# Sums of quarters of a normed activation, made in three pieces between matrix products instead of in one block ahead of them

## Chip, cores and metric

The kernel runs on one core of a Trainium2 chip. The metric is the device time of one execution in microseconds. Its time before the change is 953.83 us, the median of 3 runs (953.82 to 955.91).

## The reference, cut

One decoder layer on x of 512 tokens by 1024 channels, in float32. The part around the change:

```
h = rms_norm(x, norm_mix)
z = h @ w_in                      # split: z_rnn z_q z_k z_v z_g z_dec z_mq z_gate
out_a = rg_lru(causal_dwconv(z_rnn), ...)          # branch 0
out_b = rms_norm(chunked_gla(z_q, z_k, z_v, ...)) * silu(z_g)   # branch 1
out_c = attention of z_mq over mem                 # branch 2
proj  = einsum(branches, w_branch)                 # 768 -> 1024, for each branch
gates = sigmoid(z_gate)
x = x + (sum over branches of gates * proj) @ w_out
...                               # then a gated MLP with a conv, and a final norm
```

z_v (with the 16 columns of z_dec) and z_g are each a product of h (512 x 1024) with 768 columns.

## The kernel before

**Exact products in two halves.** TensorE (PE in the profile) multiplies rounded float32. Each operand is therefore split into an upper part and a rest by `split` (lines 96 and 97): ScalarE (ACT) copies the source to a rounded tile (`whi`, `r`), and VectorE (DVE) subtracts that from the source (`wlo`, or again `r`). `mm3` (line 103) then makes three matmuls per term: upper by upper, upper by rest, rest by upper. The normed x lies channel-major in `hh` (upper) and `hl` (rest), both finished long before the change's place.

**The products for z_v and z_g** come from `seven`: seven products of quarters stand for the eight of a 2 x 2 by 2 x 2 block product. They are called a1, a2, c1, c2, b1, b2 and b3, each in two units (p = 0 and 1) of 12 matmuls, two token tiles by six. a1 and a2 add up in the same two PSUM banks, c1 and c2 in two others, b1 to b3 in two more. After a1, `v_read` copies the banks on ACT (line 790 in the profile) before a2 adds onto them. The quarter products c1, c2, b1 and b2 need sums and differences of quarters of h on one side: `h_sums(p)` makes them on DVE for one half of the channels (p). It adds `hh` and `hl` for four quarters (line 732), makes four combinations (lines 733 to 736), and splits four results: 12 DVE operations and 4 ACT operations of 512 columns. On the weights' side, sums are made by loads that add (issued by GpSimd, line 298); a plain load goes through SyncE's queue (lines 293 and 302).

**The branches.** Branch 2 comes first, then branch 0, then branch 1. For each of the 8 blocks d of output channels a branch has a gate unit (24 matmuls of 512 columns, then a sigmoid on ACT, line 619) and a projection unit (18 matmuls, then DVE operations, lines 625 to 628). In the list `b0` of branch 0 they alternate: gate 0, projection 0, gate 1, projection 1, and so on. Projections of branch 0 need all of `oa`, the output of the LRU: `lru_square`, `lru_root` (square roots on ACT, line 695), `lru_scan` (a scan on DVE, line 708, copies on ACT, line 716, and splits).

**Order.** The program is a list of units and of steps in between. `weave(units, steps)` spreads steps behind the units of a list; `blend(units, fast)` puts a share of the made units (those of `seven`) behind each unit. A unit has hooks with a lead m: the hook is called m units ahead of it, in `emit`. Weights are loaded and split by such a hook with a lead of two (`AHEAD`). The last steps woven into the last four units of branch 2 are `lru_square` for blocks 4 to 7, `lru_root(1)`, `lru_scan` for blocks 4 to 7, and `h_sums(0)`, `h_sums(1)`. Then `blend` puts four made units behind each of the first seven units of `b0`, the 14 of z_v and then the 14 of z_g. What comes out of this is the order in which operations are handed to a planner. It puts each engine's instructions in an order of its own by when it takes them to be ready, so an engine's order can depart from the program's; on the chip each engine works through its queue in order.

**Buffers.** PSUM gives 5 banks to the big products (`bank`). Split weights have 3 buffers each for upper and rest, raw weights 4, and the 53 slots of `apool` hold activations, among them the sums (`fslot`, `rslot`).

Of the kernel before, what the change touches and what calls it, by code (L numbers as in the profile page):

```python
# [8 lines left out]
F32 = mybir.dt.float32  # L9
# [5 lines left out]
ALU = mybir.AluOpType  # L15
# [3 lines left out]
P = 128  # L19
# [12 lines left out]
LOW = 16  # L32
# [9 lines left out]
HT = S // 2  # L42
# [14 lines left out]
def trunk(ctx: ExitStack, tc: tile.TileContext, x, xT, mem, memT, par, wdecay, wch, wv, wg, wmk,  # L57
          wmv, wrg, wbr, wout, wup, wdown, wdown2, gffn, gfin, out):
    nc = tc.nc
# [11 lines left out]
    def nm(s):  # L71
        uid[0] += 1
        return f"{s}_{uid[0]}"

    def fslot(shape=(P, S)):
        return apool.tile(list(shape), F32, tag="s", name=nm("f"))

    def rslot(shape=(P, S)):
        return apool.tile(list(shape), F32R, tag="s", name=nm("r"))
# [4 lines left out]
    def bank(shape=(P, S)):  # L84
        return psm.tile(list(shape), F32, tag="mm", name=nm("mm"))
# [8 lines left out]
    def split(hi, lo, src, eng=None):  # L94

        nc.scalar.activation(hi, src, AF.Copy)  # L96
        (eng or nc.vector).tensor_tensor(out=lo, in0=src, in1=hi.bitcast(F32), op=ALU.subtract)  # L97
# [34 lines left out]
    def unit(dram, n, fn, parts=1):  # L132

        w = {}
        i = sum(1 for k, *_ in prog if k == "unit")

        def ready():
            w["w"] = fetch(dram, n, parts)
            for h in behind.get(i, ()):
                h()  # L140
        prog.append(("unit", [(AHEAD, ready)], lambda: fn(w["w"])))

    def made_unit(pre, fn):

        prog.append(("unit", pre, fn))

    def step(fn):
        prog.append(("step", [], fn))

    def weave(units, steps, lead=0):  # L150

        done, m = 0, max(1, len(units) - lead)
        for i, u in enumerate(units):
            unit(*u)
            upto = len(steps) * max(0, i + 1 - lead) // m
            for s in steps[done:upto]:
                step(s)
            done = max(done, upto)
        for s in steps[done:]:
            step(s)  # L160
# [123 lines left out]
    def seven(src, n, np, lhs, pre, read, far=AHEAD):  # L284

        raw, w, banks = {}, {}, {}

        def load(q, p):  # L290
            raw[q, p] = [fslot((P, n)) for _ in range(2)]
            for j in range(2):
                loads.append(nc.sync.dma_start(raw[q, p][j], src(q, p)[:, j, :]))

        def add(to, q, p):

            for j in range(2):
                nc.gpsimd.dma_start(raw[to, p][j], src(q, p)[:, j, :], accum_op=ALU.add)  # L298

        def direct(q, p):  # L300
            raw[q, p] = wpool.tile([P, 2, n], F32, tag="raw", name=nm("raw"), bufs=NRAW)
            loads.append(nc.sync.dma_start(raw[q, p], src(q, p)))

        def ready(key, q, p):
            hi = wpool.tile([P, 2, n], F32R, tag="whi", name=nm("whi"))
            lo = wpool.tile([P, 2, n], F32R, tag="wlo", name=nm("wlo"))
            if isinstance(raw[q, p], list):
                for j in range(2):
                    split(hi[:, j, :], lo[:, j, :], raw[q, p][j])
            else:  # L310
                split(hi, lo, raw.pop((q, p)))
            w[key, p] = hi, lo

        def run(key, p):
            ws = w.pop((key, p))
            b = key[0]
            for i in range(2):
                if key[1] == "1" and p == 0:
                    banks[b, i] = bank((P, n))
                mm3(banks[b, i], [(*lhs(key, p, j, i), ws[0][:, j, :], ws[1][:, j, :]) for j in range(2)],  # L320
                    key[1] == "1" and p == 0, p == np - 1, key[1] != "1")
                if p == np - 1:
                    read(key, i, banks[b, i])

        steps = {
            "a1": ("B11", [(6, lambda p: load("B11", p))]),
            "a2": ("B21", [(far, lambda p: direct("B21", p))]),
            "c1": ("B11", [(6, lambda p: add("B11", "B12", p))]),
            "c2": ("B22", [(far, lambda p: direct("B22", p))]),
            "b1": ("B11", [(6, lambda p: add("B11", "B22", p))]),  # L330
            "b2": ("B12", [(10, lambda p: load("B12", p)), (7, lambda p: add("B12", "B22", p))]),
            "b3": ("B11", [(6, lambda p: add("B11", "B21", p))]),
        }
        us = []
        for key, (q, before) in steps.items():
            for p in range(np):
                us.append(([(m, lambda f=f, p=p: f(p)) for m, f in before] +
                           [(AHEAD, lambda key=key, q=q, p=p: ready(key, q, p))] +
                           [(m, lambda f=f, p=p: f(p)) for m, f in pre.get(key, ())],
                           lambda key=key, p=p: run(key, p)))  # L340
        return us

    def blend(us, fast, steps=()):

        for i, u in enumerate(us):
            unit(*u)
            for l, f in ((fast, lambda v: made_unit(*v)), (steps, step)):
                for v in l[len(l) * i // len(us):len(l) * (i + 1) // len(us)]:
                    f(v)
# [4 lines left out]
    hh = hpool.tile([P, KD, S], F32R, name="hh", tag="hh")  # L354
    hl = hpool.tile([P, KD, S], F32R, name="hl", tag="hl")
# [165 lines left out]
    def proj_in(i, evac):  # L521
        return wch[i], D, lambda w: evac(channel_major(w, KD, lambda k: (hh[:, k, :], hl[:, k, :])))
# [168 lines left out]
    def lru_root(g):  # L691
        with tc.issue_after(lru["last"].ins):
            for i in range(4):
                w = lru["aw", 4 * g + i][1]
                nc.scalar.activation(w, w, AF.Sqrt)
# [23 lines left out]
                split(*rr, of[t])  # L719
                oa.append(rr)  # L720


    hsum = {}

    def h_sums(p):

        tt = nc.vector.tensor_tensor
        f = {}
        for r, c in ((2, 1), (2, 2), (1, 1), (1, 2)):
            f[r, c] = fslot((P, 2, HT))  # L730
            a, b = (v[:, 4 * c - 4 + 2 * p:4 * c - 2 + 2 * p, (r - 1) * HT:r * HT].bitcast(F32) for v in (hh, hl))
            tt(out=f[r, c], in0=a, in1=b, op=ALU.add)
        tt(out=f[2, 2], in0=f[2, 1], in1=f[2, 2], op=ALU.subtract)
        tt(out=f[2, 1], in0=f[1, 1], in1=f[2, 1], op=ALU.subtract)
        tt(out=f[1, 1], in0=f[2, 2], in1=f[1, 1], op=ALU.subtract)
        tt(out=f[1, 2], in0=f[1, 2], in1=f[1, 1], op=ALU.add)
        for key, a in (("c1", f[2, 2]), ("c2", f[1, 2]), ("b1", f[1, 1]), ("b2", f[2, 1])):
            hsum[key, p] = rslot((P, 2, HT)), rslot((P, 2, HT))
            split(*hsum[key, p], a)

    def h_lhs(key, p, j, i):
        tk = slice(i * P, (i + 1) * P)
        if (key, p) in hsum:
            return tuple(a[:, j, tk] for a in hsum[key, p])
        k = 2 * p + j + (4 if key in ("a2", "b3") else 0)
        t = 2 + i if key == "b3" else i
        return hh[:, k, t * P:(t + 1) * P], hl[:, k, t * P:(t + 1) * P]

    each = lambda fn, bs: [lambda b=b: fn(b) for b in bs]
    lo, hi = range(4), range(4, 8)  # L750
    b2 = [u for d in range(KD) for u in branch(2, oc, d)]
# [5 lines left out]
    weave([lru_weights(1)] + b2[4:8], each(lru_square, lo) + [lambda: lru_root(0)] + each(lru_split, hi))  # L757
    weave(b2[8:12], [s for p in zip(each(lru_scan, lo), each(lru_gates, hi)) for s in p])
    step(lambda: lru_decay(1))
    weave(b2[12:], each(lru_square, hi) + [lambda: lru_root(1)] + each(lru_scan, hi) + each(h_sums, range(2)))  # L760


    HP = 2 * DV
# [10 lines left out]
    def causal():  # L774
        msk = fslot((P, NT, P))
        nc.gpsimd.memset(msk, 1.0)
        nc.gpsimd.affine_select(out=msk, in_=msk, compare_op=ALU.is_ge, fill=0.0, base=0, pattern=[[0, NT], [1, P]],
                                channel_multiplier=-1)
        nc.vector.tensor_copy(mki, msk)

# [48 lines left out]
            silu(i + 2, 0, d)  # L831

    def v_fast():
        return seven(lambda q, p: wv[p, int(q[1]) - 1, int(q[2]) - 1], HP + LOW, 2, h_lhs, {}, v_read, 4)

    def g_fast():
        return seven(lambda q, p: wg[p, int(q[1]) - 1, int(q[2]) - 1], HP, 2, h_lhs, {}, g_read, 4)
# [144 lines left out]
    b0 = [u for d in range(KD) for u in branch(0, oa, d)]  # L982
    gates = {}

    def hold(d):
        def evac(ps):
            gates[d] = fslot()
            nc.scalar.activation(gates[d], ps, AF.Sigmoid)
        return proj_in(18 + 8 + d, evac)

    held = [hold(d) for d in range(KD)]
    blend(b0[:7], v_fast() + g_fast())
    weave(b0[7:] + held[:2], [decay_in, qk_back] + [lambda h=h: decay_logit(h) for h in range(H)] + [decay_log] +
          [lambda h=h: decay_apply(h) for h in range(H)])
# [325 lines left out]
```

## Time and profile before

| | us |
|---|---|
| median of 3 runs | 953.83 |
| the profiled execution | 953.96 |
| its span | 952.3 |
| PE busy | 925.5 |
| DVE busy | 637.6 |
| ACT busy | 500.4 |

A row of the timeline has start and length in us, the engine, the line, the operation, output<-inputs with shape, the count of instructions merged into it, and in brackets the idle time of the engine ahead of it and what ended that. For a matmul the inputs are named as right operand, left operand. A row of the table by stretches has the stretch and its length, then busy time and count for PE, PE's weight loads, DVE, ACT and GpSimd, then the granted clock of PE (1.00 is full), the busy share of the DMA engines, and GB/s. The mean granted clock of the execution is 0.991.

### The profile page before, as it was taken

To read this page: it belongs to the slowest core of one execution; us is meant where nothing else is said; L and a number is where in the kernel's file an instruction comes from. 1 tells how busy PE (TensorE), PEld (TensorE's weight loads), DVE (VectorE), ACT (ScalarE), POOL (GpSimd) and SP (SyncE) were. 2 spreads that over 40 slices of the span, in tenths; PEclk is the share of its full clock that TensorE was granted. 3 is DMA by queue.
4 is the path that set the end of the run, shared out by engine and by line. 5 is a ranking of instruction groups with operands and counts; after the bars stand their busy time and mean duration, and the time that the engine had idled before them with its cause. 6 is when DMAs were issued, how large, how long until landed. Compare 5 with 4: busy or idle time off the path is not lost.

```text
span 952.3 us, 12010 instructions
## 1 busy us (share of the span) xinstructions
PE 925.5 (97%) x4414; PEld 781.4 (82%) x4414; DVE 637.6 (67%) x1111; ACT 500.4 (53%) x806; POOL 82.9 (9%) x115
## 2 busy tenths in 40 slices
PE   8999999999958999999999999999999999999996
PEld 7899888888847998788888888888888888888885
DVE  7897744565785656387667674555585766689765
ACT  7664655684954444697443523343354444445544
POOL 0000000000032141000000000000020221012102
PEclk9999999999988999999999999999999999999999
DMA  7445223223276495222136701322455686357712
GB/s 251 154 130 192 85 77 98 86 87 103 73 153 149 86 215 173 83 88 73 34 96 202 239 1 45 105 95 90 157 115 147 132 212 144 111 112 184 170 45 88
DMA packets 45114, 116.09 MB, mean 122 GB/s; under 512 B 5296, under 2 KB 12608, under 8 KB 45056
## 3 DMA queue, kind: packets, MB, share of 16 engines
q1 hardware_dynamic: 33088, 94.23, 30.8%
q0 software_dynamic: 11392, 20.06, 12.5%
q10 hardware_dynamic: 576, 1.05, 0.3%
q8 instruction: 34, 0.56, 0.2%
q14 instruction: 24, 0.20, 0.1%
HBM read 111.65 MB, written 3.67 MB: 121 GB/s over the span
## 4 chain that ended last, share of the span: by engine, by line
PE 87%; ACT 5%; DVE 5%; issue 1%; DMA 0%; SPq 0%; ACTq 0%; DVEq 0%
PE mm L103 81%; PE sm L103 3%; DVE wlo L97 1%; ACT f L716 1%; PE mm L413 1%; DVE r L97 1%; ACT whi L96 1%; ACT r L96 1%; PE sm L945 1%; DMA m<-in_xT 0%; PE sm L931 0%; PE sm L947 0%; ACT L619 0%; DVE m L381 0%; PE sm L918 0%
## 5 line engine op out<-in xcount | busy, mean ns | idle before, releaser
L97 DVE TENSOR_TENSOR wlo<-raw,whi 128x1024 fp32r<-128x1024 f32 (+2 forms) x155 | 172.0, 1114 | 158.0 <-ACT whi L96 72.4
L96 ACT ACTIVATE whi<-raw 128x1024 fp32r<-128x1024 f32 (+2 forms) x155 | 149.9, 970 | 159.5 <-PE mm L103 143.8
L103 PE MATMUL mm<-whi,r 128*128 128x512 f32 (+2 forms) x568 | 171.6, 373 | 10.3 <-ACT f L619 9.6
L103 PE MATMUL mm<-h2l,whi 128*128 128x512 f32 x360 | 140.1, 389 | 0.0
L103 PE MATMUL mm<-h2h,whi 128*128 128x512 f32 x360 | 139.9, 389 | 0.0
L103 PEld LDWEIGHTS mm<-whi,r 128*128 128x128 f32 x568 | 105.7, 188 | 26.1 <-ACT f L619 10.0
L103 PE MATMUL mm<-hh,whi 128*128 128x512 f32 x288 | 113.6, 394 | 0.0
L103 PE MATMUL mm<-hl,whi 128*128 128x512 f32 x288 | 112.8, 392 | 0.0
L103 PE MATMUL mm<-wlo,r 128*128 128x512 f32 (+2 forms) x284 | 106.0, 373 | 1.2 <-DVE wlo L97 1.2
L103 PE MATMUL mm<-r,whi 128*128 128x512 f32 (+1 forms) x448 | 99.9, 373 | 2.8 <-ACT whi L96 2.8
L103 PEld LDWEIGHTS mm<-r,whi 128*128 128x128 f32 x448 | 78.5, 190 | 17.8 <-ACT whi L96 3.1
L103 PE MATMUL mm<-h2h,wlo 128*128 128x512 f32 x360 | 88.9, 389 | 0.0
L96 ACT ACTIVATE whi<-f 128x512 fp32r<-128x512 f32 (+2 forms) x90 | 48.1, 579 | 75.4 <-PE mm L103 69.1
L97 DVE TENSOR_TENSOR wlo<-f,whi 128x512 fp32r<-128x512 f32 (+2 forms) x90 | 53.7, 632 | 42.9 <-ACT whi L96 23.2
L103 PEld LDWEIGHTS mm<-h2l,whi 128*128 128x128 f32 x360 | 67.6, 188 | 14.0
L103 PEld LDWEIGHTS mm<-h2h,wlo 128*128 128x128 f32 x360 | 67.6, 188 | 14.0
L103 PEld LDWEIGHTS mm<-h2h,whi 128*128 128x128 f32 x360 | 67.5, 188 | 13.9
L1084 DVE SCALAR_TENSOR_TENSOR f<-mm,prm,f 128x511 f32<-128x511 f32 x96 | 71.4, 745 | 6.9 <-ACT f L1082 6.1
L298 POOL DMA_DIRECT2D f<-in_wdown x40 | 35.0, 976 | 435.9 <-DMA f<-in_wdown 290.9
L103 PE MATMUL mm<-hh,wlo 128*128 128x512 f32 x288 | 71.7, 390 | 0.0
L103 PEld LDWEIGHTS mm<-hh,whi 128*128 128x128 f32 x288 | 54.2, 188 | 11.7 <-issue 0.8
L103 PEld LDWEIGHTS mm<-hh,wlo 128*128 128x128 f32 x288 | 53.9, 188 | 11.1
(233 smaller groups left out, 1320.7 us busy)
## 6 DMA issues: line engine op xcount, KB each, us to landing
raw<-in_wup SPq DMA_DIRECT2D x48, 512.0 KB, 3.6
raw<-in_wch SPq DMA_DIRECT2D x40, 512.0 KB, 3.4
f<-in_wdown POOLq DMA_DIRECT2D x40, 256.0 KB, 5.6
raw<-in_wbr SPq DMA_DIRECT2D x24, 384.0 KB, 3.1
raw<-in_wdown SPq DMA_DIRECT2D x14, 512.0 KB, 3.6
f<-in_wdown SPq DMA_DIRECT2D x20, 256.0 KB, 4.9
raw<-in_wout SPq DMA_DIRECT2D x8, 512.0 KB, 3.5
f<-in_wv POOLq DMA_DIRECT2D x16, 200.0 KB, 5.1
```

Source lines behind the costliest of these rows:

```text
L96: nc.scalar.activation(hi, src, AF.Copy)
L97: (eng or nc.vector).tensor_tensor(out=lo, in0=src, in1=hi.bitcast(F32), op=ALU.subtract)
L103: nc.tensor.matmul(ps, lhsT=l, rhs=r, start=first and i == 0, stop=last and i == len(seq) - 1, skip_group_check=more)
L298: nc.gpsimd.dma_start(raw[to, p][j], src(q, p)[:, j, :], accum_op=ALU.add)
L413: nc.tensor.matmul(ps[u], lhsT=a, rhs=b, start=q == 0 and i in (0, 2), stop=q == KD - 2 and i >= len(seq) - 2)
L716: nc.scalar.activation(of[t][o:o + 32, :], gi[32 * r:32 * r + 32, :], AF.Copy)
L945: nc.tensor.matmul(ps[:, j, :], lhsT=sT[h][:, t, :], rhs=vt[t][hp][:, j, :], start=True, stop=t == 0)
L1084: nc.vector.scalar_tensor_tensor(out=a[:, j:], in0=ps[:, :S - j], scalar=col(C_FCW + 48 * (2 - j) + f), in1=a[:, j:], op0=ALU.mult, op1=AL ...
```

## The change

`h_sums(p)` is replaced by three functions. `h_sum1(p)` makes two of the quarter sums and the left operand of c1. `h_sum4(p)` makes the other two quarter sums, three combinations and the left operand of c2. `h_sum23(p)` splits the left operands of b1 and b2. They are no longer steps of the weave at the end of branch 2; they are hooks of the units of z_v: `h_sum1` with a lead of 4 ahead of c1, `h_sum4` with a lead of 5 ahead of c2, `h_sum23` with a lead of 4 ahead of b1. The operations themselves and their number are the same. The list `b0` now begins gate 0, gate 1, projection 0, projection 1, and goes on as before; so the unit between a2 and c1 is gate 1, the one between c2 and b1 is projection 0, and the one between b2 and b3 is projection 1, as before.

```
-    hsum = {}
-    def h_sums(p):
-        ...
-    weave(b2[12:], each(lru_square, hi) + [lambda: lru_root(1)] + each(lru_scan, hi) + each(h_sums, range(2)))
+    weave(b2[12:], each(lru_square, hi) + [lambda: lru_root(1)] + each(lru_scan, hi))
...
+    hsum = {}
+
+    def h_quarter(r, c, p):
+        f = hsum["f", r, c, p] = fslot((P, 2, HT))
+        a, b = (v[:, 4 * c - 4 + 2 * p:4 * c - 2 + 2 * p, (r - 1) * HT:r * HT].bitcast(F32) for v in (hh, hl))
+        nc.vector.tensor_tensor(out=f, in0=a, in1=b, op=ALU.add)
+        return f
+
+    def h_ready(key, p, a):
+        hsum[key, p] = rslot((P, 2, HT)), rslot((P, 2, HT))
+        split(*hsum[key, p], a)
+
+    def h_sum1(p):
+        a, b = h_quarter(2, 1, p), h_quarter(2, 2, p)
+        nc.vector.tensor_tensor(out=b, in0=a, in1=b, op=ALU.subtract)
+        h_ready("c1", p, b)
+
+    def h_sum4(p):
+        tt = nc.vector.tensor_tensor
+        a, b, s3, s1 = h_quarter(1, 1, p), h_quarter(1, 2, p), hsum["f", 2, 1, p], hsum["f", 2, 2, p]
+        tt(out=s3, in0=a, in1=s3, op=ALU.subtract)
+        tt(out=a, in0=s1, in1=a, op=ALU.subtract)
+        tt(out=b, in0=b, in1=a, op=ALU.add)
+        h_ready("c2", p, b)
+
+    def h_sum23(p):
+        h_ready("b1", p, hsum["f", 1, 1, p])
+        h_ready("b2", p, hsum["f", 2, 1, p])
...
     def v_fast():
-        return seven(lambda q, p: wv[p, int(q[1]) - 1, int(q[2]) - 1], HP + LOW, 2, h_lhs, {}, v_read, 4)
+        return seven(lambda q, p: wv[p, int(q[1]) - 1, int(q[2]) - 1], HP + LOW, 2, h_lhs,
+                     {"c1": [(4, h_sum1)], "c2": [(5, h_sum4)], "b1": [(4, h_sum23)]}, v_read, 4)
...
     held = [hold(d) for d in range(KD)]
+
+    b0 = b0[0:3:2] + [b0[i] for i in range(16) if i not in (0, 2)]
     blend(b0[:7], v_fast() + g_fast())
```

More of the change, by code (lines that the diff above doesn't have):

```diff
@@ L720, in lru_scan @@
                 oa.append(rr)
-    hsum = {}
-    def h_sums(p):
[L727 to L747, printed above, removed]
     each = lambda fn, bs: [lambda b=b: fn(b) for b in bs]
@@ L779, in causal, with h_lhs @@
         nc.vector.tensor_copy(mki, msk)
+    hsum = {}
[21 more added lines that the diff above has]
+        h_ready("b2", p, hsum["f", 2, 1, p])
+    def h_lhs(key, p, j, i):
+        tk = slice(i * P, (i + 1) * P)
+        if (key, p) in hsum:
+            return tuple(a[:, j, tk] for a in hsum[key, p])
+        k = 2 * p + j + (4 if key in ("a2", "b3") else 0)
+        t = 2 + i if key == "b3" else i
+        return hh[:, k, t * P:(t + 1) * P], hl[:, k, t * P:(t + 1) * P]
     def v_read(key, i, ps):
```

## The prediction

> **What bounds the kernel now.** I read the page first: TensorE (PE) is busy for nearly the whole span, so only stretches where it is idle, or slowly clocked, can give time back. The slices show one such place beside the start: slices 12 and 13, about 262 to 309 us, where its digit falls to 5 and 8 and the granted clock with it.
>
> ```profile
> PE 925.5 (97%) x4414; PEld 781.4 (82%) x4414; DVE 637.6 (67%) x1111; ACT 500.4 (53%) x806; POOL 82.9 (9%) x115
> PE   8999999999958999999999999999999999999996
> PEclk9999999999988999999999999999999999999999
> ```
>
> Then PE's timeline of that place (start, length, line, output<-right operand, left operand, count, idle time before it and what ended it).
>
> ```profile
> 254.08 2.88 PE L103 MATMUL mm<-r,whi 128*128 128x512 f32 x12
> 258.16 0.39 PE L103 MATMUL mm<-hh,whi 128*128 128x512 f32 x1
> 263.60 0.34 PE L103 MATMUL mm<-whi,hh 128*128 128x400 f32 x1
> 270.92 4.38 PE L103 MATMUL mm<-r,whi 128*128 128x512 f32 x12 [2.79 <-ACT whi L96]
> 276.89 0.35 PE L103 MATMUL mm<-whi,r 128*128 128x400 f32 x1
> 289.32 0.70 PE L103 MATMUL mm<-whi,r 128*128 128x400 f32 x1 [9.64 <-ACT f L619]
> 289.81 0.59 PE L103 MATMUL mm<-whi,hh 128*128 128x400 f32 x1
> 299.55 0.42 PE L103 MATMUL mm<-whi,r 128*128 128x400 f32 x1 [0.53 <-DVE f L798]
> 303.98 0.40 PE L103 MATMUL mm<-hh,whi 128*128 128x512 f32 x1
> 309.47 0.34 PE L103 MATMUL mm<-whi,r 128*128 128x400 f32 x1
> ```
>
> 254.08 is the last projection of branch 2, 258.16 gate 0 of branch 0, 263.60 the first product (a1), 270.92 projection 0, 276.89 the start of c1, 289.81 a2, 299.55 the end of c2, 303.98 gate 1, and 309.47 b1. PE's order is not the program's: projection 0 and a piece of c1 stand ahead of a2. Between 263.60 and 309.47, which is 45.87 us, PE does a1, a2, c1, c2, projection 0 and gate 1. At full speed these cost 4.43 for the two units of one product (299.55 to 303.98), 4.08 for a projection (254.08 to 258.16) and 5.49 for a gate (303.98 to 309.47): 4 x 4.43 + 4.08 + 5.49 = 27.3 us. So 18.6 us are lost here, and that is the most the change can bring.
>
> Who holds PE is read from the other two engines.
>
> ```profile
> 269.65 0.99 DVE L97 TENSOR_TENSOR wlo<-raw,whi 128x800 fp32r<-128x800 f32 x1 [2.40 <-ACT whi L96]
> 271.16 2.49 DVE L732 TENSOR_TENSOR f<-hh,hl 128x512 f32<-128x512 f32 x4
> 273.57 0.68 DVE L733 TENSOR_TENSOR f<-f,f 128x512 f32<-128x512 f32 x1
> 277.14 0.58 DVE L97 TENSOR_TENSOR wlo<-f,whi 128x400 fp32r<-128x400 f32 x1 [0.22 <-issue]
> 279.02 1.90 DVE L97 TENSOR_TENSOR r<-f,r 128x512 fp32r<-128x512 f32 x3 [0.21 <-ACT r L96]
> 287.77 1.90 DVE L97 TENSOR_TENSOR r<-f,r 128x512 fp32r<-128x512 f32 x3 [0.69 <-ACT r L96]
> 274.28 0.63 ACT L96 ACTIVATE r<-f 128x512 fp32r<-128x512 f32 x1 [3.42 <-DVE f L733]
> 284.40 0.63 ACT L96 ACTIVATE r<-f 128x512 fp32r<-128x512 f32 x1 [4.37 <-DVE f L733]
> 288.69 0.58 ACT L619 ACTIVATE f<-mm 128x512 f32<-128x512 f32 x1
> 289.17 0.89 ACT L790 ACTIVATE f<-mm 128x400 f32<-128x400 f32 x2
> ```
>
> Both calls of h_sums stand on DVE from 271.16 to 289.7 (287.77 + 1.90) as one block. ACT, which does the first half of each split, waits for DVE ahead of the first split of each call (3.42, 4.37), and behind the splits in its queue stand the sigmoid of gate 0 (288.69) and the two copies that read a1 (289.17). Gate 0's matmuls had ended by 263.60 and a1's before 270.92. So the 9.64 us wait on L619 is a wait for a PSUM buffer that ACT frees late because it is stuck behind h_sums; a2, which adds onto a1's banks, needs the two copies as well. The 2.79 us wait at 270.92 is projection 0 waiting for its weight split and the last LRU output.
>
> **The change part by part.** No arithmetic is added or removed: 24 DVE operations of 512 columns (16 sums, 8 lower halves) and 8 ACT halves, as before. A DVE operation takes 0.60 us in a row of them (271.16 to 273.57, four): 14.5 us in all.
>
> *The block is split.* h_sum1 (8 operations) is due four units ahead of c1, h_sum4 (12) five ahead of c2, h_sum23 (4) four ahead of b1. In the program the sigmoid of gate 0 now stands ahead of all of them, so ACT can free that bank at about 264, and a2 can follow a1. What may still stand ahead of a1's copies on ACT is the first split of h_sum1; then a2 waits for four DVE operations, 2.4 us. I cost that at nothing in the sum, because DVE works on meanwhile and DVE sets the end, as follows.
>
> *Gate 1 ahead of projection 0.* Gate 1 needs nothing but its weights. It gives PE 5.49 us while DVE makes h_sum1, and projection 0 goes behind c2, so the 2.79 us wait for the LRU output is gone: that is ready at 271.2, projection 0 now comes after 288. The cover is a2 and gate 1 together, 9.9 us. The loads change places on SP's queue.
>
> ```profile
> raw<-in_wch SPq DMA_DIRECT2D x40, 512.0 KB, 3.4
> f<-in_wv POOLq DMA_DIRECT2D x16, 200.0 KB, 5.1
> 249.96 0.33 SPq L165 DMA_DIRECT2D raw<-in_wbr  x1
> 278.01 0.86 POOL L298 DMA_DIRECT2D f<-in_wv  x1 [10.94 <-DVE wlo L97]
> ```
>
> The gate's 512 KB take the buffer that the projection's 384 KB had. The gate's load lands in 3.4 us (median), and the projection's load in that buffer was issued at 249.96, 13 us before gate 0's last matmul, so the cover is ample. The last row is POOL's queue: the accumulating load for b1 waits for c1's lower weight half on DVE. That half may come at about 282 instead of 278; b1 is wanted at about 298, so its 5.1 us landing stays hidden.
>
> *What DVE must do first.* Now DVE is the limit of this stretch. Its lower weight halves cost:
>
> ```profile
> 299.93 1.23 DVE L97 TENSOR_TENSOR wlo<-raw,whi 128x1024 fp32r<-128x1024 f32 x1
> 302.57 1.06 DVE L97 TENSOR_TENSOR wlo<-f,whi 128x400 fp32r<-128x400 f32 x2 [1.42 <-ACT whi L96]
> 297.04 1.89 DVE L97 TENSOR_TENSOR wlo<-raw,whi 128x800 fp32r<-128x800 f32 x2 [0.58 <-ACT whi L96]
> ```
>
> From 271.16 it must do, before the second unit of c2 can start: h_sum1 and h_sum4, 20 x 0.60 = 12.05; the lower weight halves of gate 1 (1.23), c1 (2 x 1.06) and c2 (1.89). That is 17.3, and with the three small waits of before (0.22 + 0.21 + 0.69 = 1.1) it ends at 289.6. Then PE has the second unit of c2 (2.2) and projection 0 (4.08): 295.9. Before, the same work ended at 309.47. Gain 13.6, against 18.6 if DVE kept up. h_sum23's four operations (2.4) fall beside projection 0 and b1 and cost nothing: the projection alone covers 4.08.
>
> *Slow clock.* PE will run into DVE at c1 or c2 with stalls of 2 to 4 us. The trace shows what follows such a stall:
>
> ```profile
> 270.90:277.00 6.10, 6.08 (x19) 4.39 (x19) 6.02 (x10) 1.60 (x3) 0.00 (x0) 0.72 0.44 131
> 289.30:292.90 3.60, 3.58 (x11) 3.45 (x12) 1.90 (x4) 0.75 (x2) 0.00 (x0) 0.52 0.02 5
> ```
>
> After the idle 2.79 us, projection 0 took 270.92 to 276.89, 5.97 against 4.08, and the granted clock of that stretch was 0.72; after the 9.64 us it was 0.52. I charge one such phase, 1.9; bounds are none (the slow phase lies beside DVE's work) and two, 3.8. The Trainium skill, in "TensorE: Matmul & The Clock Gate", in its part on the HAM clock gate, says that the clock falls back after about one idle window of 3.4 us, so that shorter gaps keep it. By that rule stalls of 2 to 3 us would cost no clock, and the sum would be 13.6 instead of 11.7, which is 940.2 and within the forecast's case. The row of 2.79 us disagrees, and I go by the row.
>
> *LRU steps.* The list woven into the last four units of branch 2 shrinks from 11 to 9 steps. Therefore lru_root moves from behind projection 6 to behind gate 7, and scans 5 and 6 from behind gate 7 to behind projection 7. I take zero: ACT had the square roots waiting on the same squares, and DVE has the idle 2.40 us (269.65) to take up work in. Bounds: a gain of 2.40 if h_sum1 fills that gap, and a loss under the third rival.
>
> *Behind it.* The gain stays to the end if later work is bound by PE.
>
> ```profile
> 264.00:272.00 8.00, 5.21 (x28) 4.70 (x27) 5.23 (x9) 6.75 (x11) 1.75 (x2) 1.00 0.58 114
> 272.00:289.40 17.40, 6.76 (x22) 4.34 (x20) 16.20 (x26) 6.18 (x12) 6.60 (x8) 0.70 0.77 168
> 289.40:297.00 7.60, 7.60 (x34) 7.46 (x34) 3.20 (x8) 3.36 (x8) 1.76 (x2) 0.78 0.07 7
> 297.00:314.00 17.00, 16.46 (x84) 14.79 (x83) 9.79 (x16) 6.29 (x12) 3.51 (x4) 1.00 0.82 194
> 314.00:367.00 53.00, 52.91 (x276) 49.50 (x277) 30.88 (x54) 22.30 (x40) 18.21 (x24) 1.00 0.74 169
> ```
>
> The row from 314 shows PE busy 52.91 of 53.00 with DVE at 58%. The DMA engines' busy time from 264 to 314 is 0.58 x 8 + 0.77 x 17.4 + 0.07 x 7.6 + 0.82 x 17 = 32.5 of 50 us; in 38 us it would be 0.85, still under 1.
>
> Sum: 13.6 - 1.9 = 11.7 us. The profiled execution took 953.96 us (its span of 952.3 and 1.66 around it), 0.13 over the median of 953.83. 953.96 - 11.7 = 942.3, and from the median 942.1.
>
> **The rivals.** *PE sets the pace.* If h_sum1 fills DVE's idle 2.40 us and the pieces fall between the splits without a stall, only 1 to 3 us of the 18.6 remain: about 937. For it: DVE is busy 16.20 of 17.40 us only because the block is there. Against: that same work still has to be done before c2.
>
> *The bubble stays.* The sums read hh and hl, which are old by then, and engines do not keep the program's order; the pieces could be set as early as before, in one block. Then only the place of projection 0 changes, and the gain is at most its 2.79: 951 to 954. Against: DVE had no free place before 269.65.
>
> *The LRU chain comes late.* The square roots now stand behind gate 7's sigmoid.
>
> ```profile
> 250.25 1.16 ACT L695 ACTIVATE f<-f 96x512 f32<-96x512 f32 x2
> 254.27 1.28 ACT L619 ACT_TABLE_LOAD   x1
> 264.75 0.88 ACT L96 ACTIVATE whi<-raw 128x800 fp32r<-128x800 f32 x1
> ```
>
> Gate 7's matmuls end at 254.08, so roots that began at 250.25 would begin at about 256 (0.6 for the sigmoid, 1.28 for a table), and ACT's following chain, with the weight splits of a2 in it (264.75), slips by up to 5.8 less the load saved ahead of the sigmoid, 1.28: 4.5. The gain is then 11.7 - 4.5 = 7.2, or 946.6. The Trainium skill, "ScalarE: Activation LUTs", section "What ACT_TABLE_LOAD costs", gives 2.66 us for a switch of tables; an estimate from that page would be a loss larger by 1.4 for a further switch, while the row at 254.27 shows 1.28.
>
> *Slower: six stalls in place of one.* Each of the six calls (three pieces, two halves of the channels) has its ACT half waiting on DVE in an in-order queue that also frees PSUM. If none of them ran beside matmuls, PE would lose 14.5 for DVE, 6 x 0.6 for ACT's halves and 6 x 1.9 for slow clock, 29.5 against 18.6 now: 965. It decides when less than about a third of that, 10.9 of 29.5, is hidden. Against it: a2 and gate 1 need none of the sums and cover 9.9 by themselves.
>
> **How the numbers follow.** Forecast (gain 9 to 16, around 942.1) 0.62; PE sets the pace 0.12; LRU chain late (gain 4 to 9) 0.14; bubble stays 0.06; six stalls 0.06. A change below 0.3%, 2.9 us, can hardly be told from none. Faster 0.88, same 0.06, slower 0.06. The range takes in the first three, from 936 (17.8 gained) to 949 (4.8 gained).
>
> **What would show it.** Right: the sigmoid of gate 0 soon after 264; a2 directly behind a1; DVE's sums in several places instead of one block; stalls of PE at c1 or c2 ended by DVE; b1 starting near 298. Wrong: the 9.64 us wait back on L619 or L790, square roots behind 255 with the a2 splits late, or PE's stalls at each of c1, c2, b1 and b2.

## The result, and the profile after

The changed kernel takes 948.25 us (median of 4 runs, 947.32 to 949.42) against 953.83 (4 runs, 953.26 to 955.91): 5.6 us less. The ratio is 0.9938, with a 95% interval of 0.9918 to 0.9958. So it is faster by more than 0.3% over the whole interval, and by half of the 11.7 us that was forecast. Its profiled execution took 949.42 us, the upper end of its runs. When this kernel was measured a second time (below), one of five executions took 1160.11 us at a mean granted clock of 0.751; it is left out there.

The page of the changed kernel: busy times, then the slices.

```profile
PE 925.9 (98%) x4414; PEld 782.4 (83%) x4414; DVE 636.8 (67%) x1111; ACT 500.4 (53%) x806; POOL 83.0 (9%) x115
PE   8999999999987999999999999999999999999996
PEclk9999999999998999999999999999999999999999
```

The hole of before (digits 5 and 8) has become an 8 and a 7. Work is the same. The next fence is PE's timeline of that place.

```profile
263.64 0.34 PE L103 MATMUL mm<-whi,hh 128*128 128x400 f32 x1
271.15 0.50 PE L103 MATMUL mm<-hh,whi 128*128 128x512 f32 x1 [2.98 <-ACT whi L96]
277.89 0.35 PE L103 MATMUL mm<-whi,hh 128*128 128x400 f32 x1
293.65 3.33 PE L103 MATMUL mm<-r,whi 128*128 128x512 f32 x7 [6.26 <-DVE f L805]
296.77 0.54 PE L103 MATMUL mm<-whi,r 128*128 128x400 f32 x1
302.26 1.32 PE L103 MATMUL mm<-r,whi 128*128 128x512 f32 x5
304.80 0.34 PE L103 MATMUL mm<-whi,r 128*128 128x400 f32 x1
322.34 0.33 PE L103 MATMUL mm<-whi,hh 128*128 128x384 f32 x1
```

263.64 is the start of a1, 271.15 gate 1, 277.89 a2. c1 follows and ends at about 287.4. Then PE stands still for 6.26 us until 293.65, where projection 0 begins; 296.77 is c2, 302.26 the rest of projection 0, and b1 starts at 304.80 instead of 309.47. The last row is the first matmul of z_g. The same row of before is:

```profile
327.02 0.33 PE L103 MATMUL mm<-whi,hh 128*128 128x384 f32 x1
```

Both kernels have done the same units by that row, so the stretch from the start of a1 to it measures the place by itself: 327.02 - 263.60 = 63.4 us before, 322.34 - 263.64 = 58.7 after. That is 4.7 us, and the profiled executions differ by 4.5: what was gained here was kept to the end.

Two waits are left, 2.98 and 6.26 us. ACT and DVE show what they are.

```profile
268.76 0.87 ACT L96 ACTIVATE whi<-raw 128x800 fp32r<-128x800 f32 x1
270.06 1.04 ACT L96 ACTIVATE whi<-raw 128x1024 fp32r<-128x1024 f32 x1
271.00 0.58 ACT L619 ACTIVATE f<-mm 128x512 f32<-128x512 f32 x1
274.57 0.63 ACT L96 ACTIVATE r<-f 128x512 fp32r<-128x512 f32 x1 [2.99 <-DVE f L769]
277.21 0.88 ACT L801 ACTIVATE f<-mm 128x400 f32<-128x400 f32 x2
292.06 0.63 ACT L96 ACTIVATE r<-f 128x512 fp32r<-128x512 f32 x1 [3.79 <-DVE f L777]
292.60 0.85 ACT L804 ACTIVATE f<-mm 128x384 f32<-128x384 f32 x2
279.98 0.57 DVE L97 TENSOR_TENSOR wlo<-f,whi 128x400 fp32r<-128x400 f32 x1 [2.12 <-PE mm L103]
286.43 0.69 DVE L97 TENSOR_TENSOR r<-f,r 128x512 fp32r<-128x512 f32 x1
291.34 0.69 DVE L777 TENSOR_TENSOR f<-f,f 128x512 f32<-128x512 f32 x1
292.72 0.69 DVE L97 TENSOR_TENSOR r<-f,r 128x512 fp32r<-128x512 f32 x1 [0.69 <-ACT r L96]
293.33 0.33 DVE L805 COPY f<-mm 128x16 f32<-128x16 f32 x2
```

The 6.26 us are not a wait for the sums of c2 as such: the left operand of c2's first unit is complete at 287.1 (286.43 + 0.69). PE has projection 0 next in its queue, and that needs a PSUM bank. The banks of a2 come free by its two reads, L804 on ACT and L805 on DVE (the lines were 793 and 794 before). a2 had ended by 282.3. But in ACT's queue L804 stands behind the last split of h_sum4, which waits 3.79 us for DVE, and L805 stands behind the same split on DVE. That the bank is what projection 0 waits for is read from the order here; the run with a sixth bank below tests it. It is the fault of before, a read stuck behind sums, one product later. The 2.98 us are gate 1 waiting for its weight split (270.06), the end of ACT's chain of LRU copies. a2 could not fill that gap: in PE's order it stands behind gate 1, and it needs the copies of a1 (L801). These came at 277.21, behind h_sum1's first split (274.57); without that split they could not have begun before the sigmoid was done either (271.00 + 0.58), which is after the gap. In sum1_early below they come at 271.14, and the wait is the same.

```profile
271.10:277.80 6.70, 6.65 (x22) 5.24 (x23) 5.97 (x10) 2.15 (x5) 0.00 (x0) 0.75 0.59 183
293.60:299.40 5.80, 5.75 (x16) 5.08 (x17) 3.48 (x7) 2.42 (x5) 1.76 (x2) 0.51 0.99 321
```

In this table by stretches the granted clock is the third number from the end: both waits are followed by slow clock, 0.75 and 0.51.

### The profile page after: what moved, and what is told of

The parts are those of the page before. It is cut to its first block, busy times and chain, and to the rows that moved or that the text cites. A ratio compares the mean times of both kernels' runs of the same rounds, so it can differ in the third digit from the quotient of the medians.

```text
span 947.7 us, 12014 instructions
## 1 busy us (share of the span) xinstructions
PE 925.9 (98%) x4414; PEld 782.4 (83%) x4414; DVE 636.8 (67%) x1111; ACT 500.4 (53%) x806; POOL 83.0 (9%) x115
## 4 chain that ended last, share of the span: by engine, by line
PE 88%; ACT 5%; DVE 5%; issue 1%; DMA 0%; SPq 0%; DVEq 0%; ACTq 0%
PE mm L103 81%; PE sm L103 3%; DVE wlo L97 1%; ACT f L716 1%; PE mm L413 1%; ACT whi L96 1%; DVE r L97 1%; PE sm L957 1%; ACT r L96 0%; DMA m<-in_xT 0%; PE sm L943 0%; PE sm L959 0%; ACT L619 0%; DVE m L381 0%; PE sm L930 0%
## 5 line engine op out<-in xcount | busy, mean ns | idle before, releaser
L96 ACT ACTIVATE whi<-raw 128x1024 fp32r<-128x1024 f32 (+2 forms) x155 | 150.0, 970 | 162.0 <-PE mm L103 148.9
L96 ACT ACTIVATE whi<-f 128x512 fp32r<-128x512 f32 (+2 forms) x90 | 48.2, 580 | 74.9 <-PE mm L103 62.9
L103 PEld LDWEIGHTS mm<-hl,whi 128*128 128x128 f32 x288 | 54.7, 190 | 11.1
```

The costliest lines, as they stand in the source:

```text
L103: nc.tensor.matmul(ps, lhsT=l, rhs=r, start=first and i == 0, stop=last and i == len(seq) - 1, skip_group_check=more)
```

## The experiments

*Queue theory*: the missing part of the gain is lost because reads that free PSUM stand behind the sums' splits in the in-order queues of ACT and DVE. *DVE theory*: DVE delivers the sums at its rate whatever the order. A *stretch* below is the time from the first matmul of a1 to the first of z_g in the profiled execution; times are medians; ratios are against the kernel before on the same chip, with a 95% interval.

| kernel | stretch, us | time, us | ratio, interval |
|---|---|---|---|
| before | 63.4 | 953.8 to 954.6 | 1 |
| changed | 58.7 | 948.25 | 0.9938, 0.9918 to 0.9958 |
| changed, again | 58.9 | 948.2 | 0.9935, 0.9921 to 0.9948 |
| gates_only | 62.5 | 954.66 | 0.9998, 0.9989 to 1.0007 |
| pieces_only | 57.0 | 945.41 | 0.9912, 0.9897 to 0.9928 |
| no_sums | 50.0 | 940.44 | 0.9853, 0.9839 to 0.9866 |
| sum4_late | 53.4 | 945.27 | 0.9911, 0.9897 to 0.9924 |
| banks6 | 56.6 | 949.14 | 0.9949, 0.9936 to 0.9963 |
| reads_ahead | 54.9 | 945.13 | 0.9899, 0.9886 to 0.9913 |
| copies_pool_reads | 58.3 | 948.85 | 0.9940, 0.9927 to 0.9952 |
| copies_late | 59.4 | 950.00 | 0.9959, 0.9946 to 0.9971 |
| copies_late2 | 59.4 | 950.58 | 0.9963, 0.9954 to 0.9972 |
| old_order_late | 56.2 | 948.34 | 0.9936, 0.9924 to 0.9949 |
| sum1_early | 49.4 | 941.56 | 0.9871, 0.9854 to 0.9887 |

The profiled execution is not the median one (that of pieces_only took 948.82 us, its longest, that of sum1_early 939.73, its shortest), so a stretch and a median beside it need not agree to the microsecond.

**The two halves of the change.** gates_only is the kernel before with the new list b0; pieces_only is the changed kernel without it.

```
gates_only (on before):    + b0 = b0[0:3:2] + [b0[i] for i in range(16) if i not in (0, 2)]
pieces_only (on changed):  - b0 = b0[0:3:2] + [b0[i] for i in range(16) if i not in (0, 2)]
```

> The kernel before with the new order of branch 0's units alone (gate 0, gate 1, projection 0); the sums stay one block at the end of branch 2. If the loss is in the queues (ACT and DVE keep the reads that free PSUM banks behind the sums): gate 1 runs in the first gap, but the sigmoid of gate 0 and the copies of a1 still stand behind the whole block, so a wait of some 9 us stays and b1 starts about 1.4 us sooner than before's 309.47: 951 to 954 us. If the place of projection 0 was what mattered: the 2.79 us wait and its slow clock go, 4.7 us: 949.

> The changed kernel with branch 0's units in the old order; only the sums are in three pieces. Queue theory: the 9.64 us wait is gone, projection 0 waits some 2.8 us in the first gap as before, and a unit that needs a PSUM bank still waits for a2's reads behind the second part of the sums: most of the change's 5.6 us, 947 to 950. If the new order of units carries the change: 952 to 954.

The order of units alone brings nothing that can be measured (954.66 against 954.42 for before on the same chip). Its trace shows what the first case said: the wait on the sigmoid of gate 0 is still there, 9.15 us, with the sums still in one block. The pieces alone bring 9 us, more than expected (947 to 950), and their trace shows where they differ from the changed kernel:

```profile
288.77 0.70 PE L103 MATMUL mm<-whi,r 128*128 128x400 f32 x1 [9.15 <-ACT f L619]
288.62 0.50 PE L103 MATMUL mm<-hh,whi 128*128 128x512 f32 x1 [1.15 <-ACT whi L96]
295.06 0.85 ACT L804 ACTIVATE f<-mm 128x384 f32<-128x384 f32 x2
```

The first row is of gates_only, the other two of pieces_only. There a2's reads on ACT (L804, 295.06) are as late as in the changed kernel (292.60), but the next unit, gate 1, starts at 288.62 after a wait of only 1.15 us, and not for a bank. A bank was free for it, most likely projection 0's, which DVE had read at 281.54 (L627); in the changed kernel the unit in that place is gate 1, whose reader is the sigmoid on ACT, and that ran only at 293.34, behind the same split as the reads of a2. Which bank is given to which unit the trace does not say, so this reason is argued, not shown.

The changed kernel, which has both, brings less than the pieces, and so it did when it was run again:

> The changed kernel once more, beside the next three on one chip, to see whether it really lies above the kernel with the pieces alone (945.4). If the order of units costs something: 947 to 949 again. If that was scatter between runs: 945 to 946.

It took 948.2 us again, in the range of the first case. The intervals of pieces_only and the changed kernel overlap a little, so I take it as likely, not shown, that the new order took back some 3 us.

**Without the sums.**

```
-                     {"c1": [(4, h_sum1)], "c2": [(5, h_sum4)], "b1": [(4, h_sum23)]}, v_read, 4)
+                     {}, v_read, 4)
```

> The changed kernel without the sums: c1, c2, b1 and b2 take plain quarters of h where the sums should stand, so 24 DVE and 8 ACT operations are left out. Queue theory and DVE theory alike: no wait on the sums is left; the wait of about 3 us ahead of gate 1 (or a2), behind ACT's chain of LRU copies, stays with its slow clock of 1.9, so b1 starts at 263.6 + 27.3 + 4.9 = 295.8 instead of 304.8: 939 to 940 us. If something else also bounds the stretch (loads, or weight splits): above 943. If the forecast's 18.6 us were all to be had: 935.

It came out as both theories expect, 940.4 (0.4 above their range). The 3 us wait is still there though no sum is (PE: gate 1, and the first matmul of z_g):

```profile
271.42 0.50 PE L103 MATMUL mm<-hh,whi 128*128 128x512 f32 x1 [2.99 <-ACT whi L96]
313.93 0.33 PE L103 MATMUL mm<-whi,hh 128*128 128x384 f32 x1
```

So of the 18.6 us that the prediction counted as lost, about 5 (18.6 less the 13.4 by which the stretch is now shorter than before; this wait and its slow clock) never belonged to the sums. That they belong to ACT's chain of LRU copies is tested further below.

**h_sum4 later.** The piece comes behind a2's reads in the program; nothing else changes.

```
-                     {"c1": [(4, h_sum1)], "c2": [(5, h_sum4)], "b1": [(4, h_sum23)]}, v_read, 4)
+                     {"c1": [(4, h_sum1)], "c2": [(3, h_sum4)], "b1": [(4, h_sum23)]}, v_read, 4)
```

> The changed kernel with h_sum4's lead cut from 5 to 3, so that in the program, and by the planned order on ACT, a2's two reads stand ahead of h_sum4's splits instead of behind them. DVE's amount of work is unchanged and c2's operand comes no sooner. Queue theory: projection 0's 6.26 us wait for the bank goes, and other work fills PE until c2: 4 to 6 us less than the changed kernel, 942 to 944. DVE theory (DVE's rate of delivering the sums is the limit whatever the order): c2 waits instead, within 1.5 us of the changed kernel, 947 to 950.

PE and ACT:

```profile
271.39 0.50 PE L103 MATMUL mm<-hh,whi 128*128 128x512 f32 x1 [2.99 <-ACT whi L96]
286.80 3.06 PE L103 MATMUL mm<-r,whi 128*128 128x512 f32 x12 [0.71 <-ACT whi L96]
293.72 0.58 PE L103 MATMUL mm<-whi,r 128*128 128x400 f32 x1 [2.51 <-ACT r L96]
279.99 0.49 ACT L804 ACTIVATE f<-mm 128x384 f32<-128x384 f32 x1
281.86 0.48 ACT L804 ACTIVATE f<-mm 128x384 f32<-128x384 f32 x1
292.52 1.67 ACT L96 ACTIVATE r<-f 128x512 fp32r<-128x512 f32 x3 [1.66 <-DVE f L777]
```

and the table row behind the first wait:

```profile
271.40:277.50 6.10, 6.10 (x28) 5.15 (x29) 5.37 (x10) 2.76 (x6) 0.00 (x0) 1.00 0.56 182
```

The reads L804 now come at 279.99 and 281.86 instead of 292.60, projection 0 starts at 286.80, and the 6.26 us wait is 0.71. The last split of h_sum4 comes no sooner (292.52; it was 292.06), and PE waits for an ACT half of the sums for 2.51 us behind projection 0. The stretch is 5.3 us shorter; 1.7 of it is the clock, which stayed at 1.00 behind the first wait in this execution (0.75 in the changed kernel: 22 matmuls of gate 1 in 6.74 us against 22/24 x 5.49 = 5.03). So 3.6 us, against 3.0 by the medians. The time, 945.27, lies between the ranges of the two theories (942 to 944, 947 to 950), and each is right in part. Order alone moved it, with DVE's amount of work the same: the wait for the bank is gone, and four of its five runs (944.27 to 946.04) are faster than all eight of the changed kernel (946.98 to 949.42), though the intervals overlap a little. DVE's rate is seen too, as the 2.51 us that follow.

**A sixth bank.**

```
-    psm = pool("psm", 5, space=PSUM)
-    pss = pool("pss", 3, space=PSUM)
+    psm = pool("psm", 6, space=PSUM)
+    pss = pool("pss", 2, space=PSUM)
```

> The changed kernel with six PSUM banks for the big products and two instead of three for the small ones; the places of the sums are unchanged. Queue theory with the bank as the thing waited for: projection 0 takes the sixth bank, the 6.26 us wait on a2's read goes, and the stretch from the first matmul of a1 (263.6 in the changed kernel) to the first of z_g's a1 (322.3), 58.7 us, shortens by 4 to 6; elsewhere two small banks may cost some us. DVE theory: PE waits for c2's operand instead, the stretch shortens by less than 2.

PE's timeline:

```profile
288.18 3.02 PE L103 MATMUL mm<-r,whi 128*128 128x512 f32 x12 [0.93 <-ACT whi L96]
295.06 0.28 PE L856 MATMUL sm<-ident,f 128*16 128x128 f32 x1 [2.49 <-DVE f L805]
```

Projection 0 starts at 288.18, so the bank was indeed what it waited for. But the read L805 is as late as before, and the next one in PE's queue that needs its result, a small transpose of the decay's input, waits for it instead. The stretch falls by 2.1 us, between the two expectations, and the kernel's time not at all. From the first matmul of z_g to the end of its span it takes 626.9 us (947.0 - 320.11), where the changed kernel takes 625.4 (947.7 - 322.34): most of the 2.1 us is lost again behind the stretch. Whether that is for want of the small bank is open.

**Splits held behind a1's copies.** On sum4_late.

```
-                     {"c1": [(4, h_sum1)], ...
+                     {"c1": [(3, h_sum1)], ...
-            nc.scalar.activation(gla["k", i], ps, AF.Copy)
+            gla["read"] = nc.scalar.activation(gla["k", i], ps, AF.Copy)
     def h_ready(key, p, a):
-        split(*hsum[key, p], a)
+        with tc.issue_after(gla["read"].ins):
+            split(*hsum[key, p], a)
```

> The kernel with h_sum4's lead at 3, and h_sum1's at 3 too, and the ACT halves of all these splits held behind a1's copies in ACT's queue. In the planned order a2 now follows a1 after four matmuls of gate 1. Queue theory: a2 no longer waits for gate 1, but ACT's chain of LRU copies still ends at 270, so the 3 us wait there stays; c1's operand comes later, by up to 1.3 us; 943 to 946, no better than h_sum4's lead alone by more than 1.5. If a1's copies behind the first split were the larger half of what is left (against the 940.4 without sums): 941 to 943.

945.13, as the first case said: the reads of a1 behind the first split cost next to nothing. In the changed kernel gate 1 runs while they are late.

**ACT's chain of LRU copies.** Three kernels try to remove the 3 us wait: the copies made by GpSimd (on reads_ahead), or queued behind a1's copies on ACT (on reads_ahead, and on sum4_late).

```
copies_pool_reads:
-            nc.scalar.activation(of[t][o:o + 32, :], gi[32 * r:32 * r + 32, :], AF.Copy)
+            nc.gpsimd.tensor_copy(of[t][o:o + 32, :], gi[32 * r:32 * r + 32, :])
copies_late, copies_late2 (the copies leave lru_scan for a function lru_out):
+    def lru_outs(p):
+        with tc.issue_after(gla["read"].ins):
+            for b in (4 + 2 * p, 5 + 2 * p):
+                lru_out(b)
-                     {"c1": [(4, h_sum1)], ...
+                     {"c1": [(4, h_sum1), (2, lru_outs)], ...      (copies_late: 3 for h_sum1)
```

> The same with the twelve LRU copies (0.64 us each on ACT) made by GpSimd. If ACT's chain sets the 3 us wait at 268 and its slow clock: both go, about 4.9 us, 939 to 941. If GpSimd's copies are slow or hold its accumulating loads up (c1 then waits for its weights): 944 or above.

> The kernel reads_ahead with the twelve LRU copies (and the splits of the LRU's output) queued on ACT behind a1's copies instead of ahead of them; projection 0, which needs them, comes behind c1. If ACT's chain of copies sets the 3 us wait at 268: a2 follows a1 at once, the wait and its slow clock go, the stretch from a1 to z_g's a1 (54.9 there, 53.4 with h_sum4's lead alone) falls to about 50, 940 to 942 us. Rival: ACT only does the same work later, ahead of a2's reads and projection 0; the stretch stays at 53 or more, 944 to 947.

> The same move of the LRU copies on the kernel sum4_late, where h_sum1 keeps its lead of 4 and no split is held behind a1's copies. By the first theory 941 to 943, with a1's copies behind the first split of h_sum1 (up to 1 us); by the rival 944 to 947.

In all three the 2.98 us wait is gone, and larger ones have come. Of copies_pool_reads, GpSimd's copies and what ACT waits for:

```profile
263.66 5.46 POOL L716 COPY f<-f 32x512 f32<-32x512 f32 x4
269.15 0.63 ACT L96 ACTIVATE r<-f 128x512 fp32r<-128x512 f32 x1 [4.92 <-POOL f L716]
```

Four copies take 5.46 us where ACT took 2.56 (before, at 262.16), and ACT's in-order queue now waits for them. Of copies_late, ACT, DVE and PE:

```profile
284.69 2.55 ACT L718 ACTIVATE f<-f 32x512 f32<-32x512 f32 x4
287.94 0.69 DVE L97 TENSOR_TENSOR r<-f,r 128x512 fp32r<-128x512 f32 x1 [2.28 <-ACT r L96]
299.28 0.70 PE L103 MATMUL mm<-whi,r 128*128 128x400 f32 x1 [8.72 <-ACT r L96]
```

The copies are now late for the last split of the LRU's output, DVE waits 2.28 us for it with both calls of h_sum4 queued behind, and PE waits 8.72 us. The rival of these expectations held, and more than held: 950.00 and 950.58 us, against 944 to 947. So ACT's chain sets the 3 us wait, but moving the chain costs more than the wait.

**The old order with h_sum4 late.** sum4_late without the new list b0.

> The kernel sum4_late (h_sum4's lead at 3) with branch 0's units in the old order. If the new order of units is worth nothing, or costs, once the pieces are placed (as gates_only and pieces_only say): 943 to 946, no slower than sum4_late's 945.3. If it is worth its 9.9 us of cover: above 947.

948.34, 3 us slower than sum4_late and in the range of the second case. With h_sum4 late the new order of units is worth 3 us (their intervals just touch, and the stretches differ by 2.8); with h_sum4 early it likely cost as much. The worth of gate 1's place depends on where the reads stand.

The same run also limits the queue theory. Beside pieces_only it differs only in h_sum4's lead, as sum4_late does beside the changed kernel. There the later h_sum4 gained 3.0 us; here it gained nothing, and by the medians it even cost 2.9 (948.34 against 945.41, intervals that overlap a little). ACT and PE of old_order_late, then PE of pieces_only:

```profile
282.04 0.47 ACT L804 ACTIVATE f<-mm 128x384 f32<-128x384 f32 x1
295.15 0.45 PE L103 MATMUL mm<-whi,r 128*128 128x400 f32 x1 [3.60 <-ACT r L96]
296.26 0.39 PE L856 MATMUL sm<-ident,f 128*16 128x128 f32 x2 [1.90 <-DVE f L805]
```

The reads are early now (282.04 against 295.06), but PE gets on no sooner. It waits 3.60 us for a half of the sums and resumes at 295.15, 31.6 us behind its first matmul of a1 (263.59). In pieces_only it waits 1.90 us for a read behind the sums and resumes at 296.26, 31.5 us behind a1 (264.79). In the old order the sums hold PE up wherever the reads stand. What makes the 2.9 us between the medians is open.

**h_sum1 early.** On sum4_late; h_sum1 leaves the hooks and is woven into branch 2, some 50 us earlier.

```
-                     {"c1": [(4, h_sum1)], "c2": [(3, h_sum4)], "b1": [(4, h_sum23)]}, v_read, 4)
+                     {"c2": [(3, h_sum4)], "b1": [(4, h_sum23)]}, v_read, 4)
-    weave([lru_weights(1)] + b2[4:8], each(lru_square, lo) + [lambda: lru_root(0)] + each(lru_split, hi))
+    weave([lru_weights(1)] + b2[4:8], each(lru_square, lo) + [lambda: lru_root(0)] + each(lru_split, hi) + each(h_sum1, range(2)))
```

> The kernel sum4_late with both calls of h_sum1 taken out of the stretch: they are steps woven into an earlier part of branch 2, where DVE is busy 10 to 13 of every 20 us and their 8 operations (4.9 us) and 4 ACT halves lie beside matmuls. In the planned order ACT then has nothing of the sums ahead of the reads of a1 and a2. If DVE's and ACT's load inside the stretch is what is left between sum4_late (stretch 53.4 us, 945.3) and the kernel without sums (50.0, 940.4): two thirds of the 2.51 us wait and of the slow clock go, stretch 50.5 to 52, 941.5 to 943.5 us. If only the order of the queues counted and sum4_late has it right already: 945. If DVE's work only comes to stand in another critical place (before the LRU's scans), or the eight buffers held longer stop something: 946 or more.

DVE, ACT and PE:

```profile
217.29 1.28 DVE L727 TENSOR_TENSOR f<-hh,hl 128x512 f32<-128x512 f32 x2
271.14 0.89 ACT L801 ACTIVATE f<-mm 128x400 f32<-128x400 f32 x2
263.30 0.34 PE L103 MATMUL mm<-whi,hh 128*128 128x400 f32 x1
270.81 0.50 PE L103 MATMUL mm<-hh,whi 128*128 128x512 f32 x1 [2.99 <-ACT whi L96]
312.72 0.33 PE L103 MATMUL mm<-whi,hh 128*128 128x384 f32 x1
```

The table row behind the wait of 2.99 us:

```profile
270.80:276.00 5.20, 5.19 (x27) 4.99 (x28) 2.80 (x7) 2.69 (x6) 0.87 (x2) 1.00 0.85 284
```

The first sums stand at 217.29, a1's copies come straight behind the sigmoid (271.14 instead of 277.21), and only the 2.99 us wait and two under 0.8 are left. The stretch is 49.4 us. The kernel takes 941.56 us, 12.8 less than before beside it (954.39), ratio 0.9871 (0.9854 to 0.9887): the fastest that does all the work, and 1 to 2 us from the kernel without sums (940.44, ratio 0.9853). It fell into the first case of the expectation, with a stretch even shorter than the 50.5 to 52 named there.

## Why the prediction came out as it did

The direction and the range (936 to 949) held; the gain was 5.6 us where 11.7 were forecast. The reading of before was right in the main: the 9.64 us wait came from reads stuck behind the block of sums, since it stays with the block (gates_only, 9.15 us) and goes with the pieces. The main forecast, a gain of 9 to 16 with a chance of 0.62, failed. 5.6 us lies in the band of the rival "the LRU chain comes late" (4 to 9), but that is luck: its mechanism did not happen, and the 6.1 us that are missing were lost in other ways.

- *The 18.6 us as the most to be had*: the arithmetic of that place was right, but I gave all of it to the sums and the wait of projection 0 on the LRU output. Without the sums 50.0 us of stretch remain, 13.4 less than before. The rest is mostly ACT's chain.
- *"The 2.79 us wait for the LRU output is gone"*: wrong. It came back at the same moment as 2.98 us ahead of gate 1. The row of before named it (ACT, a weight split). I had named the weight split beside the LRU output and then kept only the latter, while any unit whose weights are split at the end of that ACT chain meets the wait.
- *"a2 can follow a1", the sigmoid "at about 264"*: wrong. The sigmoid ran at 271.00 behind the LRU copies, and a1's copies at 277.21 behind h_sum1's first split. The risk of the split I had named and priced at nothing; reads_ahead confirms the price. The chain stood in the trace of before, on ACT without a pause from 254.27 until 270.87:

  ```profile
  266.17 2.55 ACT L716 ACTIVATE f<-f 32x512 f32<-32x512 f32 x4
  270.04 0.83 ACT L96 ACTIVATE whi<-raw 128x768 fp32r<-128x768 f32 x1
  ```
- *DVE ends at 289.6*: it ended at 293.4 (292.72 + 0.69), 3.8 later. It stood idle 2.12 us up to 279.98, by its row for a weight buffer that PE still held, which my sum by busy times left out, and projection 0's own weight split came ahead of the last sums.
- *The step that failed most*: that PE would do c2's first unit while DVE still works, and then have only c2's second unit and projection 0 left. The planned order put projection 0 ahead of c2, and it needed a bank held by a2's reads behind h_sum4. So from 293.65 PE still had both units of c2 and projection 0 before it: 4.43 + 4.08 + 2.6 of slow clock = 11.1 to b1 at 304.80, instead of 2.2 + 4.08 + 1.9 = 8.2. With DVE's 3.8 this is 6.7 of the 7.0 us by which b1 was later than the forecast 297.8. sum4_late shows the order's part by itself: about 3 us.
- *One phase of slow clock, 1.9*: there were two, 1.7 behind the first wait and 2.6 behind the second, together 4.3 and over the upper bound of 3.8 that was kept for two.
- *LRU steps at zero, loads and GpSimd's queue hidden*: right as far as the trace shows; the last square root began at 253.68 (before: 253.64), and no wait of PE in this place ends on a load.
- *The rivals*: six stalls did not come, the bubble did not stay in its place. It moved from a1's reads to a2's, which none of the rivals said; "stuck behind h_sums" was in my reading of before and I did not ask which read would be next.

## What to carry to other kernels

When a block of side work is cut into pieces and put between products, look at each piece for what stands behind it in its engine's queue, above all the reads that free accumulators. Where the unit that comes next on TensorE needs one of those accumulators, the piece belongs behind the reads; where it does not, this order gains nothing (old_order_late). The order in the engine's queue, not in the program, decides. Work whose inputs are old is better put where its engine is half idle than just ahead of its use: here taking a third of the sums 50 us forward brought 3.7 us, setting the next half behind the reads of a2 3.0, in the new order of units.

## What the runs showed of the hardware

The same idle gap did not always cost clock. A gap of 2.98 or 2.99 us at the same place was followed by a granted clock of 0.75 in the changed kernel and of 1.00 in sum4_late and sum1_early (rows above). Between the changed kernel and sum4_late that is 1.7 us of time. The prediction weighed a rule of the Trainium skill ("TensorE: Matmul & The Clock Gate", part on the HAM clock gate) against the one gap of 2.79 us and went by the row. That part also says that the activity window runs freely; two outcomes at one place would fit with that, but no run here shows that this is the reason. What does not fit is the length: a gap of 2.51 us (sum4_late, ahead of 293.72) was followed by a granted clock of 0.53 as well, and all these gaps are shorter than the idle window of 3.4 us that the Trainium skill gives for the fall.

```profile
293.70:297.00 3.30, 3.28 (x10) 3.24 (x11) 3.21 (x6) 0.49 (x1) 0.43 (x1) 0.53 1.13 261
```

GpSimd's copy of 32 x 512 took 1.37 us (5.46 for four), where ACT takes 0.64 (2.56 for four). It was not always so slow: the last four, from 269.96 on, took 3.63, and DVE stood idle for 1.8 us of that.
